# Output weights split in two steps of four, and short side work taken together in one step

## Chip, cores and metric

The kernel runs on one core of one Trainium2 chip. The metric is the device time of one execution in microseconds (us); the median of several executions counts, and lower is better.

## What is computed

One step of a hybrid decoder with one layer: a prompt of 1024 rows and eight single-row decodes (1032 rows together, `NT`). The normalized input is projected by `w_in`; three mixers follow (sparse attention with compressed, selected and window branches, a causal pooling mixer, a gated spatial mixer); each is widened by a SiLU gate; the three outputs are joined and go through one output projection.

```python
def pool_mix(xin, prev, pos0, w_pool, scale):
    ...
    diff = (jnp.concatenate(pooled, axis=-1) - xf[:, POOL_MAX - 1:]).reshape(b, t, N_POOL_GROUPS, POOL_GROUP_DIM)
    y = jnp.einsum('btgc,gce->btge', diff, w_pool).reshape(b, t, D_POOL)
    return y * scale

def merge_groups(x, ya, za, yb, zb, yc, zc, w_out, g_post):
    mix = jnp.concatenate([ya * jax.nn.silu(za), yb * jax.nn.silu(zb), yc * jax.nn.silu(zc)], axis=-1)
    out = jnp.einsum('bte,ed->btd', mix, w_out)
    return x + rms_norm(out, g_post).astype(x.dtype)
```

## The kernel before, in words

Every fp32 operand is split into a high and a low fp16 part, and a product is three matmuls (high by high, low by high, high by low).

The second part of the kernel, from about 205 us on, is one loop over 50 units of attention (`units`, `st` counts the steps). Prompt rows come in tiles of 128 in the order 7, 6, 2, 1, 0, 5, 4, 3 (`ROWS`); a unit is one, two or four heads of a tile. Steps 0 to 7 are tile 7, 8 to 15 tile 6, 16 to 19 tile 2, 20 to 23 tile 1, 24 and 25 tile 0, 26 to 33 tile 5, 34 to 41 tile 4, 42 to 49 tile 3. A step writes, in this order: the scores of its unit (`qk`: matmuls `s`, VectorE's `P` with the row minimum, ScalarE's exponential on `P`, ScalarE's high part `H`), VectorE's low part `L` of the unit before with its DMA transpose (`low`, L1365), the DMA transpose of this unit's `H` (`high`, L1357), one round of the background tasks (`bg_step`), a helping of other work (`take`), and the matmuls `O` with the values for the unit three steps back (`pv`), with `combine` at the end of a half tile and `finish` at the end of a tile.

`take(budget)` draws from two lists. `side` holds `dec_mix`, `gmlp(0)`, `gmlp(1)`, `poolmm(1)`, `poolmm(0)`, `dec_out`; `fill` holds the last groups of the input projection (`tgroup`: ZC1, U1, PIN1, ZB1, PIN0, ZB0, in this order, three chunks of 3.5 each), `early_wo`, `open_out`, and then one `outproj(i)` for each finished tile. Each is a generator that writes a chunk and names its price; the price 0 means that it waits for something. The budget of a step is what is owed (never above 0) plus 6.2 until `open_out` has run, and plus 0.52 times the unit's size after, less 0.19 times the size; the size is 12 in tile 2, 8 in tiles 1, 0 and 3, 11 in tile 5. `take` first draws one chunk of `side`, whatever the budget is, then chunks of `fill` while the budget is above 0 and fewer than two chunks with a PSUM bank to be emptied were drawn. What empties a bank is put in `posts` and written when the next chunk has been written, or at the start of the next step; what comes after it (`fin`) is a background task and goes on in the next `bg_step`. `now` is the planner's own clock, `later` a clock of GpSimd's work on it.

`poolmm(f2)` is one half of the pooled products: three chunks of price 0.45 over 344 columns each, three matmuls `pp` into one bank of the pool `fp`, emptied by VectorE at L1202 into `yzb`; then `fin`: the high part of `mxp` by ScalarE (L1188), the low part by GpSimd (L1189), and `mxp0` or `mxp1` is there. `poolmm(1)` waits for `dh1` (GpSimd's last subtraction of the pooling task `post_pin(1)`, L1171) and for the gate `zb1`; `poolmm(0)` likewise for `dh0` and `zb0`.

`fp` has two banks of PSUM for all this: the groups `ps`, `pp`, `op` (output projection), `oc` (compressed attention, `cmp_out`), `mp` (the transposes in `finish`), `dops` (`dec_out`).

`open_out` runs once ZB0's last chunk is written. It gives back the room of the input, clears a tile on GpSimd (L1447) and starts `split_wo`: seven loads of 512 KB of output weights `wor1` to `wor7` and one of `gpb` on GpSimd's queue (`wor0` came by `early_wo`), then in later rounds the splits `wo`: ScalarE's high part (L1483) and VectorE's low part (L1484). The order of the eight weights is `forder` = 6, 7, 5, 4, 0, 1, 2, 3: 6 and 7 meet `mxg`, 5 meets `mxp1`, 4 meets `mxp0`, 0 to 3 the attention. A weight may be used from the round after its split. `outproj(i)` takes two halves of 512 columns, eight weights by three matmuls `op`; weight 4 goes last where `mxp0` isn't there. While fewer than eight weights are there, each weight is a chunk of 0.65. `dec_out` needs all `mxp`, all weights.

The SP and GpSimd queues are kept in the order of the code (`manual_schedule`); the order on TensorE, VectorE and ScalarE is arranged by the framework at build time.

Of the kernel before, what the change touches and what calls it, by code (L numbers as in the profile page):

```python
# [50 lines left out]
def tile_hymba(ctx: ExitStack, tc: tile.TileContext, A: dict):  # L51
# [40 lines left out]
    def flush():  # L92
        while posts:
            run_post(posts.pop(0))
# [42 lines left out]
    def chunk(gen):  # L137
        r = next(gen, None)
        if r is None:
            return None  # L140
        flush()
        if r[1] is not None:
            posts.append(r[1])
        now[0] += r[0]
        return r[0]
# [454 lines left out]
    def dec_cmp():  # L600
        add_pe(0)
        add_pe(1)
        prep("c", 0)
        yield 0, None
        for b in range(8):
            if b < 6:
                add_pe(b + 2)
            if b < 7:
                prep("c", b + 1)
            else:  # L610
                prep("k", 0)
            hl = chl.pop(("c", b))
            yield compress([(r, hl, r * 512, ms[:, r, b * 8:b * 8 + 8]) for r in range(2)], f"d{b}", f"cd{b}")
# [623 lines left out]
    def small():  # L1237
        yield from small_w()
        for q in range(3):
            nxt_load()  # L1240
        yield 0, None
# [4 lines left out]
    side = [small(), dec_cmp()]  # L1246
# [196 lines left out]
    def open_out():  # L1443
        X.release()
        outp["O"] = tc.alloc_tile_pool(name="O", bufs=1, side="left", reuse_waits="tile")
        outp["one"] = outp["O"].tile([128, 128], F32, name="one2")
        G.memset(outp["one"], 1.0)  # L1447
        bg.append(split_wo())
        yield 0.1, None
# [8 lines left out]
    def load_wo(q):  # L1458
        O = outp.get("O")
        if q == 0:  # L1460
            t = RW.tile([128, 1024], F32, tag="raw", name="wor0", bufs=1)
        elif q < 6:
            t = O.tile([128, 1024], F32, tag=f"w{q + 2}", name=f"wor{q}", bufs=1)
        else:
            t = O.tile([128, 1024], F32, tag="xr", name=f"wor{q}", bufs=2)
        wor[q] = t
        later(0.6)
        G.dma_start(t, A["wo"][forder[q]])

    def split_wo():  # L1470
        for q in range(1, 8):
            load_wo(q)
        outp["gpb"] = outp["O"].tile([128, 1024], F32, name="gpb")
        G.dma_start(outp["gpb"], A["gpb"])
        for part in ((0, 1, 2), (3, 4, 5), (6, 7)):
            yield
            for q in list(outp):
                if q in range(8):
                    wo[forder[q]] = outp.pop(q)
            for q in part:  # L1480
                raw = wor.pop(q)
                w = outp["O"].tile([128, 2, 1024], F16, tag=f"w{q}", name=f"wo{q}", bufs=1)
                S.activation(w[:, 0], raw, AF.Copy, scale=64.0)  # L1483
                V.scalar_tensor_tensor(w[:, 1], raw, 64.0, w[:, 0], ALU.mult, ALU.subtract)  # L1484
                outp[q] = w
        yield
        for q in part:
            wo[forder[q]] = outp.pop(q)
# [118 lines left out]
    side = []  # L1607

    def take(budget):
        banks = 0  # L1610
        c = 0
        while side and c == 0:
            c = chunk(side[0])
            if c is None:
                side.pop(0)
                c = 0
            elif c == 0:
                break
        if c:
            budget -= c  # L1620
            banks = 1
        while budget > 0 and fill and banks < PARAM["banks"]:
            c = chunk(fill[0])
            if c is None:
                fill.pop(0)
                continue
            if c == 0:
                break
            banks += len(posts) > 0
            budget -= c  # L1630
        return min(budget, 0.0)
# [9 lines left out]
    for st in range(n + 3):  # L1641
        t0 = now[0]
        flush()
        u = units[st - 1] if 1 <= st <= n else None
        if st < n:
            pend[units[st]] = qk(units[st])
        if u is not None:
            pend[u] = low(u, *pend[u])
        if st < n:
            pend[units[st]] = high(units[st], *pend[units[st]])  # L1650
        bg_step()
        if st >= n:
            bg_step()
            take(5.2)
        else:
            i, s0, nh = units[st]
            size = nh * (i + 1 + min(i + 1, 5))
            now[0] += 0.19 * size
            owed = take(owed + (PARAM["s2"] * size if "O" in outp else PARAM["s1"]) - 0.19 * size)
            now[0] = max(now[0], t0 + 0.33 * size + 0.8)  # L1660
        if st >= 3:
            v = units[st - 3]
            pv(v, pend.pop(v))
            e = v[1] + v[2]
            if e % 4 == 0:
                run_post(lambda: combine(v[0], v[1] // 4))
            if e == 8:
                fill.append(outproj(v[0]))
    while fill or side:
        flush()  # L1670
        bg_step()
        bg_step()
        take(1.0)
        now[0] += 1.0
# [165 lines left out]
```

## Time and profile before

| | us |
|---|---|
| median of 3 executions | 579.41 |
| the three | 579.08, 579.41, 589.81 |
| the profiled execution | 582.92 |
| its span, first to last instruction | 581.2 |

PE is TensorE's matmuls, PEld its weight loads, DVE is VectorE, ACT ScalarE, POOL GpSimd, SP the queue that issues most DMAs. A row of a timeline has start, duration, engine, line, operation, out<-in with shape, the count of merged instructions, and in brackets the idle time before it and what ended that. Idle times of an engine count only where the engine, or what waits for it, sets the end. Line 67 is the helper that writes every matmul, so matmuls are told apart by their tiles.

### The profile page before, as it was taken

Reading aid. Unit: us, or ns where it says so; the run is one execution under the profiler, and the core shown is the slowest. Engines: PE = TensorE matmul, PEld = TensorE weight load, DVE = VectorE, ACT = ScalarE, POOL = GpSimd, SP = SyncE. Lnnn points to the kernel's source line nnn. Section 1 sums busy time; section 2 is a strip of 40 time slices with the busy share of each in tenths; the row PEclk is TensorE's granted clock in tenths of the full one; section 3 lists DMA queues with packets and bytes.
Section 4 is the critical chain, followed back from the end, with each engine's and each line's share of the span. In section 5 each row is a group of like instructions: output and inputs, shape, how many; then the busy total and the mean of one; then the engine's idle time right before and its main releaser. Section 6 shows DMA issues by size and latency. Waiting matters only on the chain. (4 is left out here: it accounts for less than half of the span.)

```text
span 581.2 us, 14266 instructions
## 1 busy us (share of the span) xinstructions
PE 524.4 (90%) x5748; PEld 347.0 (60%) x5748; DVE 447.1 (77%) x747; ACT 323.4 (56%) x574; POOL 197.5 (34%) x157
## 2 busy tenths in 40 slices
PE   5889989899999999899999888957587999999985
PEld 3556645479877999766666556533345555555452
DVE  5986389998687568469887897869889777888842
ACT  7444144555534434348666666678777566766620
POOL 1894187502266200043937785223000110000000
PEclk9999997999999999999999989975778999999998
DMA  8613984665776111748987588899859899899870
GB/s 297 265 37 111 246 220 126 183 197 160 212 261 178 38 39 21 188 108 172 186 161 143 118 144 149 130 308 156 127 118 143 119 195 200 184 175 204 169 196 36
DMA packets 191125, 93.29 MB, mean 161 GB/s; under 512 B 160458, under 2 KB 179434, under 8 KB 191058
## 3 DMA queue, kind: packets, MB, share of 16 engines
q1 hardware_dynamic: 187170, 78.82, 62.4%
q0 software_dynamic: 3744, 13.29, 7.1%
q8 instruction: 45, 0.74, 0.5%
q10 hardware_dynamic: 144, 0.26, 0.1%
q14 instruction: 22, 0.18, 0.1%
HBM read 45.49 MB, written 11.86 MB: 99 GB/s over the span
## 5 line engine op out<-in xcount | busy, mean ns | idle before, releaser
L67 PE MATMUL ps<-xh,ws 128*128 128x344 f16 x768 | 179.1, 316 | 7.9 <-DVE ws L261 2.6
L67 PEld LDWEIGHTS <-ws 128*128 128x128 f16 x1376 | 129.2, 100 | 90.4 <-issue 16.1
L1348 ACT ACTIVATE P<-P,sm 128x640 f32<-128x640 f32 (+7 forms) x128 | 92.8, 726 | 73.6 <-DVE sm L1346 73.3
L67 PE MATMUL ps<-xl,ws 128*128 128x344 f16 x384 | 121.3, 316 | 0.0
L1364 DVE SCALAR_TENSOR_TENSOR L<-P,H 128x1024 f16<-128x1024 f32 (+4 forms) x50 | 88.8, 1775 | 20.1 <-ACT H L1350 18.5
L1346 DVE CUSTOM_DVE_ANT_0 P<-s,ctt 128x640 f32<-128x640 f32 (+7 forms) x128 | 84.8, 699 | 8.9 <-PE s L67 8.5
L67 PEld LDWEIGHTS <-qa 128*128 128x128 f16 (+1 forms) x612 | 44.7, 98 | 59.6 <-issue 33.5
L67 PE MATMUL O<-vn,T 128*128 128x64 f16 x1584 | 62.2, 197 | 12.3 <-DMA T<-L 8.3
L67 PEld LDWEIGHTS <-T 128*128 128x128 f16 x1584 | 57.4, 101 | 25.2 <-DMA T<-L 9.1
L1350 ACT ACTIVATE H<-P 128x1024 f16<-128x1024 f32 (+4 forms) x50 | 66.2, 1325 | 1.0
L67 PEld LDWEIGHTS <-xh 128*128 128x128 f16 x768 | 60.2, 98 | 0.7
L67 PE MATMUL s<-ka,qa 128*128 128x384 f16 (+4 forms) x192 | 44.2, 330 | 5.0 <-DVE sm L1346 4.7
L67 PE MATMUL op<-wo,qa 128*128 128x512 f16 x192 | 45.1, 381 | 0.5 <-DVE wo L1484 0.5
L67 PE MATMUL zps<-ws,xh 128*128 128x128 f16 x512 | 45.0, 219 | 0.0
L67 PE MATMUL zps<-ws,xl 128*128 128x128 f16 x256 | 43.6, 219 | 0.0
L1514 POOL TENSOR_SCALAR sq<-sq 128x1 f32<-128x1 f32 x8 | 4.2, 528 | 112.1 <-ACT o L1546 112.1
L67 PEld LDWEIGHTS <-xl 128*128 128x128 f16 x384 | 37.5, 98 | 1.1 <-issue 0.5
L255 ACT ACTIVATE ws<-raw 128x1024 f16<-128x1024 f32 x21 | 22.2, 1056 | 17.1 <-PE ps L67 11.9
L67 PE MATMUL s<-klx,qx 64*128 64x384 f16 (+4 forms) x92 | 26.4, 327 | 4.2 <-DMA qx<-qa 4.2
L67 PE MATMUL s<-kl,qa 64*128 64x384 f16 (+5 forms) x100 | 29.1, 334 | 0.0
L67 PE MATMUL op<-wo,mxg 128*128 128x512 f16 x96 | 25.5, 403 | 2.2 <-DVE yzb L1202 2.2
L1073 POOL TENSOR_TENSOR t<-t,yzc 128x1032 f32<-128x1032 f32 x2 | 4.8, 2382 | 61.5 <-DMA qx<-qa 61.0
(335 smaller groups left out, 924.1 us busy)
## 6 DMA issues: line engine op xcount, KB each, us to landing
raw<-in_wt_dram SPq DMA_DIRECT2D x21, 512.0 KB, 4.6
wor<-in_wo_dram POOLq DMA_DIRECT2D x8, 512.0 KB, 9.4
xr<-in_xn_dram SPq DMA_DIRECT2D x8, 512.0 KB, 4.1
o_y_dram<-o SPq DMA_DIRECT2D x7, 512.0 KB, 3.3
cr<-in_ccmp_dram SPq DMA_DIRECT2D x24, 128.0 KB, 2.8
o_kww_dram<-in_cwin_dram POOLq DMA_DIRECT2D x8, 259.0 KB, 4.1
o_kww_dram<-in_cwin_dram POOLq DMA_DIRECT2D x8, 252.0 KB, 4.4
xq<-in_xT_dram SPq DMA_DIRECT2D x3, 516.0 KB, 7.0
```

Of the source, the lines that this page charges most:

```text
L67: nc.tensor.matmul(out, lhsT=l, rhs=r, start=st, stop=en)
L255: S.activation(ws[:, 0, :, a:b], r, AF.Copy, scale=64.0)
L1073: G.tensor_tensor(t, t, hold.pop(f"zc{f2}"), ALU.mult)
L1346: V.tensor_tensor_reduce(p, ps[:, z:z + T], ctt[:, end - T:end], -slope, 3e38, ALU.add, ALU.min, sm[:, s, br:br + 1])
L1348: S.activation(p, p, AF.Exp, bias=sm[:, s, br:br + 1], scale=-1.0, accum_out=sm[:, s, 2 + br:3 + br])
L1350: S.activation(H, P, AF.Copy, scale=1024.0)
L1364: V.scalar_tensor_tensor(L, P, 1024.0, H, ALU.mult, ALU.subtract)
L1514: G.tensor_scalar(sq[:, 2:3], sq[:, 1:2], 1.0 / 1024, sq[:, 0:1], ALU.mult, ALU.add)
```

## The change

`split_wo` splits the weights in two rounds of four instead of three rounds of three, three and two. `take` draws chunks of `side` until their prices reach 1.0, instead of one chunk; a chunk of price 0 ends it as before. Of the side tasks, `gmlp` has chunks of 1.4 and `dec_out` chunks of 2.6, 2.6 and 0.2; only the three chunks of 0.45 of a `poolmm` are short enough to come together.

```diff
-        for part in ((0, 1, 2), (3, 4, 5), (6, 7)):
+        for part in ((0, 1, 2, 3), (4, 5, 6, 7)):
...
-        while side and c == 0:
-            c = chunk(side[0])
-            if c is None:
+        while side and c < 1.0:
+            d = chunk(side[0])
+            if d is None:
                 side.pop(0)
-                c = 0
-            elif c == 0:
+                continue
+            if d == 0:
                 break
+            c += d
```

## Rows read from the trace of the kernel before

**Rows 1.** The page: busy time, share of the span and count of instructions of three engines.

```profile
PE 524.4 (90%) x5748; PEld 347.0 (60%) x5748; DVE 447.1 (77%) x747; ACT 323.4 (56%) x574; POOL 197.5 (34%) x157
```

**Rows 2.** Busy time by stretch: start and end, length, then PE, PEld, DVE, ACT and POOL busy with counts, the granted TensorE clock as a share of full speed, the DMA engines' busy share, GB/s.

```profile
366.00:377.00 11.00, 10.63 (x130) 6.67 (x128) 10.98 (x26) 6.30 (x14) 0.23 (x2) 1.00 0.76 125
377.00:390.00 13.00, 6.19 (x52) 3.92 (x51) 7.55 (x14) 8.16 (x18) 4.17 (x8) 0.74 1.08 283
390.00:413.00 23.00, 17.79 (x165) 9.17 (x166) 22.95 (x52) 19.29 (x44) 6.18 (x3) 0.70 0.91 167
413.00:430.00 17.00, 12.09 (x132) 7.08 (x129) 12.75 (x50) 11.73 (x40) 0.00 (x0) 0.60 0.70 101
430.00:444.00 14.00, 8.93 (x105) 4.76 (x101) 13.86 (x25) 11.96 (x20) 2.15 (x1) 1.00 0.85 166
444.00:454.75 10.75, 10.63 (x208) 7.91 (x207) 9.58 (x19) 7.36 (x14) 1.25 (x1) 0.68 1.15 141
454.75:561.90 107.15, 107.15 (x1073) 57.31 (x1070) 81.75 (x150) 64.30 (x126) 8.19 (x15) 1.00 0.91 180
561.90:581.20 19.30, 10.85 (x44) 4.75 (x42) 6.27 (x10) 1.97 (x5) 0.81 (x2) 0.84 0.23 82
```

**Rows 3.** SP's queue in the timeline: the transpose of H in steps 19, 25 and 28, which mark how far attention is, and the store of the pooling state.

```profile
373.75 0.62 SPq L1163 DMA_DIRECT2D o_ps_dram<-dsh  x1
...
395.05 1.47 SPq L1357 DMA_TRANSPOSE T<-H  x1
...
429.16 1.23 SPq L1357 DMA_TRANSPOSE T<-H  x1
...
443.64 1.66 SPq L1357 DMA_TRANSPOSE T<-H  x1
```

**Rows 4.** The timeline around the first half's pooled products, `poolmm(1)`, and the start of the output projection: matmuls `pp`, `op`, `oc`, VectorE's L1202, the last part of ZB0 (L492).

```profile
367.60 0.61 PE L67 MATMUL pp<-mxp,wpl 128*128 128x344 f16 x3
369.01 3.04 PEld L67 LDWEIGHTS <-ws 128*128 128x128 f16 x22
370.69 0.57 DVE L1202 SCALAR_TENSOR_TENSOR yzb<-pp,psc,yzb 128x344 f32<-128x344 f32 x1
375.79 0.51 DVE L492 SCALAR_TENSOR_TENSOR t<-ps,R 128x344 f32<-128x344 f32 x1
383.33 1.06 PE L67 MATMUL pp<-mxp,wpl 128*128 128x344 f16 x3
387.14 0.63 PE L67 MATMUL pp<-mxp,wpl 128*128 128x344 f16 x3
389.39 0.57 DVE L1202 SCALAR_TENSOR_TENSOR yzb<-pp,psc,yzb 128x344 f32<-128x344 f32 x1
390.01 1.30 PE L67 MATMUL op<-wo,mxg 128*128 128x512 f16 x4 [2.25 <-DVE yzb L1202]
```

**Rows 5.** POOL's queue in the timeline from the pooling task's last work before `open_out` on.

```profile
364.32 1.04 POOL L1141 TENSOR_TENSOR ab<-ab 64x512 f32<-64x512 f32 x1
376.42 0.20 POOL L1447 MEMSET one<- 128x128 f32 x1 [11.07 <-DVE t L492]
376.97 3.68 POOL L1468 DMA_DIRECT2D wor<-in_wo_dram  x7 [0.35 <-PE s L67]
393.70 2.65 POOL L1189 TENSOR_TENSOR mxp<-yzb,mxp 128x1032 f16<-128x1032 f32 x1 [12.53 <-ACT mxp L1188]
396.31 2.66 POOL L1171 TENSOR_TENSOR mxp<-ab,mxp 128x512 f16<-128x512 f32 x1
```

**Rows 6.** DVE in the timeline: `L` of 1536 columns and a split of `wo`, each once without and once with GpSimd at work.

```profile
387.72 1.75 DVE L1364 SCALAR_TENSOR_TENSOR L<-P,H 128x1536 f16<-128x1536 f32 x1
393.17 1.17 DVE L1484 SCALAR_TENSOR_TENSOR wo<-wor,wo 128x1024 f16<-128x1024 f32 x1
394.26 3.69 DVE L1364 SCALAR_TENSOR_TENSOR L<-P,H 128x1536 f16<-128x1536 f32 x1
397.88 2.17 DVE L1484 SCALAR_TENSOR_TENSOR wo<-wor,wo 128x1024 f16<-128x1024 f32 x1
```

**Rows 7.** The three longest idle times of ACT, PE and DVE between 375 and 385 us, in the timeline.

```profile
381.84 0.22 ACT L1162 ACTIVATE dsh<-t 128x8 f32<-128x8 f32 x1 [6.14 <-DMA o_ps_dram<-dsh]
382.11 0.39 PE L67 MATMUL s<-klx,qx 64*128 64x256 f16 x1 [4.21 <-DMA qx<-qa]
384.23 1.23 DVE L1059 SCALAR_TENSOR_TENSOR yzb<-yzb,t 128x1032 f32<-128x1032 f32 x1 [5.42 <-ACT yzb L1056]
```

**Rows 8.** The splits: the two lines over the span (duration least/median/most, first and last start), the time of the loads from issue to landing, and the second and the last of ACT's rows.

```profile
L1483 ACT ACTIVATE wo<-wor x8: 1039/1040/1057, 384.1 to 405.3; 128x1024 f16<-128x1024 f32 x8
L1484 DVE SCALAR_TENSOR_TENSOR wo<-wor,wo x8: 1172/1218/2172, 385.4 to 409.1; 128x1024 f16<-128x1024 f32 x8
DMA to landing us min/median/max: 5.9/9.4/12.0
389.30 1.99 ACT L1483 ACTIVATE wo<-wor 128x1024 f16<-128x1024 f32 x2
```

**Rows 9.** The timeline of the second half's pooled products, `poolmm(0)`, and of what waits for it.

```profile
427.04 1.05 PE L67 MATMUL pp<-mxp,wpl 128*128 128x344 f16 x3
433.25 0.52 DVE L1202 SCALAR_TENSOR_TENSOR yzb<-pp,psc,yzb 128x344 f32<-128x344 f32 x1
433.83 0.82 PE L67 MATMUL oc<-vbd,pct 128*128 128x256 f16 x6 [1.35 <-DVE yzb L1202]
435.01 2.15 POOL L1189 TENSOR_TENSOR mxp<-yzb,mxp 128x1032 f16<-128x1032 f32 x1 [27.61 <-ACT mxp L1188]
436.98 0.38 PE L67 MATMUL op<-wo,mxp 128*128 128x512 f16 x1
444.22 0.35 PE L67 MATMUL dops<-md,wo 128*128 128x16 f16 x8
454.78 1.46 PE L67 MATMUL op<-wo,mxg 128*128 128x512 f16 x6
```

**Rows 10.** The end: the last transpose of L on SP, and the last `O` and the last tile's projection on PE.

```profile
556.37 1.70 SPq L1365 DMA_TRANSPOSE T<-L  x1
561.02 0.81 PE L67 MATMUL O<-vn,T 128*128 128x64 f16 x22
569.50 5.34 PE L67 MATMUL op<-wo,qa 128*128 128x512 f16 x24
```

## The prediction

> **What bounds the kernel now.** I read the page first, then busy time by stretch, then the waits between 370 and 450 us, and at last the timeline there, on SP's and POOL's queues and around every tile that the diff touches. The page calls PE 90% busy [rows 1], an average over three stages. From 454.75 to 561.9 us PE is busy without a gap at the full clock [rows 2]: whatever is left of the output projection then costs its own length. From 377 to 444 PE has gaps: 6.19 of 13, 17.79 of 23, 12.09 of 17, 8.93 of 14 us busy, at a granted clock of 0.60 to 0.74 up to 430 [rows 2]. There VectorE fills 390 to 413 (22.95 of 23 us). After 561.9 the last tile's chain runs alone. So the change, which lies at 367 to 455 us, is worth what it lets PE do in the gaps, and each us gained there reaches the end.
>
> The engines don't keep the code's order: the first pooled product is written in step 19 and ran at 367.60 [rows 4], while SP issued step 19's transpose at 395.05 [rows 3]. Side work runs up to 27 us ahead where its data and one of the two `fp` banks are there. At 427 to 444 it runs level with attention (the products of step 24 and after beside step 25's transpose at 429.16, step 28's `dops` at 444.22 beside its transpose at 443.64) [rows 3, 9].
>
> **The change, part by part.**
>
> *Planner.* Step 18 writes two chunks of ZB0 on a budget of 6.2 - 0.19 x 12 = 3.92, so step 19 owes 3.08 and has 0.84. Before: one product (0.45) leaves 0.39, and ZB0's last chunk is written too. After: three (1.35) leave -0.51; that chunk moves to step 20, whose 6.2 - 1.52 - 0.51 = 4.17 holds it, and `open_out` stays there. `mxp1` comes in the round of step 20 instead of 22. `dh0` stays at step 24 (GpSimd's planned clock reaches 344.49, step 23 starts at 344.19). `poolmm(0)` is then written in step 24 alone instead of 24 to 26; all weights are there at step 24, not 25; `mxp0` at 26 instead of 28. `dec_out` and the end of `outproj(7)`'s first half move from step 28 to 26, and every later piece of the projection stands two steps earlier.
>
> *poolmm(1), 367 to 397 us.* Its products ran at 367.60, 383.33, 387.14; after the last, VectorE's L1202 at 389.39 freed the bank for which `op` waited 2.25 us [rows 4]. All three will now run near 368 to 372. GpSimd's L1189 then stands behind L1141 (ended 365.4) and ahead of the clearing and the seven loads, which ran at 376.42 and 376.97 [rows 5]. It runs near 374 instead of 393.70, and L1171, queued behind it, near 384 instead of 396.31. That frees VectorE: beside those two, an `L` took 3.69 us instead of 1.75 and a split 2.17 instead of 1.17 [rows 5, 6]. 1.94 + 1.00 = 2.9 us leave the stretch in which VectorE is full. The 2.25 us of PE lie in the same stretch and aren't added: **-2.9**. Bounds: -5.1 (both), and 0 (the price moves along, below).
>
> *What that costs at 366 to 379.* VectorE is full there too (10.98 of 11) [rows 2]: it gets two L1202 (2 x 0.57) and what L1189 takes from it. On PE, the third product waits for the first one's bank (freed 371.26, the end of L1202 at 370.69), and ZB0's last chunk, which ran from 369.01, for the next: its end at 375.79 moves by about 2.5 us, and with it the clearing and all loads on POOL [rows 4, 5]. Up to 1.1 + 2.5 = 3.7 us; taken as **0**, since right behind stand idle times of 6.14 us on ACT, 4.21 on PE and 5.42 on DVE [rows 7]. With that cover gone it costs 3.7. It may even gain: the store that ACT waits for was issued at 373.75 [rows 3], 3.2 us ahead of the loads, and took 8 us beside them; with the loads later, those waits may shrink, at most by 4.2.
>
> On a rule against this: the Trainium skill (SBUF — State Buffer, Who interferes with whom) says that a VectorE instruction with two SBUF inputs and a GpSimd one that reads SBUF exclude each other, the later one waiting for the whole of the earlier. By it the price isn't removed but goes with L1189 to its new place, so the term would be about -0.3, not -2.9. The trace shows such a wait in the old place alone.
>
> *The splits.* Still eight by 1.04 us on ACT and 1.2 on DVE [rows 8]: 0 for the work. Four in the first round need `wor3`, the last four `wor7` one round sooner. Loads are issued by 376.97 + 3.68 = 380.65 and take at most 12.0 [rows 5, 8]: landed by 392.7, or 395.2 with the 2.5 us above. The second split ran at 389.30 with no wait for a load, the last at 405.3. The eighth may come at 400; the second may wait. Cost **0**; 2.5 us if ACT stands at the second split until its load lands, with all exponentials behind it.
>
> *poolmm(0), 427 to 455 us.* From the first product to the end of the last L1202: 427.04 to 433.77, 6.7 us, in one bank, because `op` of tile 7 holds the other until `mxp0` [rows 9]. Three products in a row at 0.84 us (mean of the four groups shown: 0.61, 1.06, 0.63 [rows 4], 1.05) plus 0.57 of L1202 are 4.2. `mxp0`, `op` at 436.98 and `dops` follow: **-2.5**. Bounds: 0 (other DVE work still goes between), and -7.3: two steps of tile 5 with 0.33 x 11 = 3.6 of projection each, all done in PE's gaps. `dops` at 444.22 stands behind step 28's work and may now go ahead of it; I take the near end, since the data (`mxp0`) and the bank decide here.
>
> *Sum.* -2.9 + 0 + 0 - 2.5 = -5.4 against the profiled execution: 582.9 - 5.4 = 577.5. That execution stands 3.5 above the median of the runs, so 574.0.
>
> **Rivals.**
>
> *A, swallowed:* the order of work changes and the time doesn't. For it: 427 to 444 is held up by VectorE too (13.86 of 14) [rows 2], and at the end the last `O` (561.02) waits for the transpose issued at 556.37, while `op` of tile 4 fills the wait; projection done earlier leaves that wait empty [rows 10]. The lock rule above ends here as well. Against: PE is full for 107 us before that. Gain 0 to 2: 577.4 to 579.4.
>
> *B, slower:* the weights come late. ZB0's last chunk must wait for two L1202, and the clearing and the loads wait for it on POOL. Price 2.5 us of load plus 2.5 of ACT standing at a split: 584. It decides once the loads start after about 380. For it: the loads saturate DMA (1.08 busy) [rows 2]. Against: the last split had 12 us to spare. Price up to 10 if step 18's transposes fall into the burst anew.
>
> *C, larger:* the waits of rows 7 shrink by 4.2 and PE keeps its clock. From 444 to 454.75 PE is busy 10.63 us at 0.68 [rows 2]; at 1.00 that is 7.2, 3.4 less. 574.0 - 4.2 - 3.4 = 566.4. Against: both need gaps to vanish that have other causes. The Trainium skill (TensorE: Matmul & The Clock Gate, What's actually happening) says the array runs at 1.2 GHz after idling and 2.4 when kept busy; the stretches of rows 2 agree.
>
> *D, no change of order* is excluded: the budget of step 19 alone moves a chunk.
>
> **How the numbers follow.** Forecast, 571 to 577: 0.42. A, 577 to 580: 0.27. B, 580 to 592: 0.19, of it 0.09 above 584. C, 564 to 571: 0.12, of it 0.05 below 567. The likeliest gives 574.0; 567 to 584 leaves out 0.14. Two per cent, about what a measurement can tell from no change, is 11.6 us: below 567.8 lie 0.07, above 591 lie 0.05, between 0.88. The likeliest's own range is 571 to 577, all inside "same".
>
> **What would show it.** Right: three groups of `pp` between 367 and 374; L1189 of the first half ahead of the loads; no `L` of 1536 columns above 3 us after 390; `mxp0`'s L1189 near 432.6; `dops` by 441; the gapless stretch of PE starting about 5 us sooner. Wrong: loads after 380 with ACT idle ahead of a split; the waits of rows 7 as long or longer; a new wait of PE for `T` after 430; or PE idle longer at 556 to 565 by what was gained.

## The result, and the profile after

The changed kernel takes 591.02 us (median of 4 executions, 589.28 to 594.29) where the kernel before takes 581.27 in the same comparison (the three executions of the table and one of 583.13): a ratio of 1.0144, interval 1.0102 to 1.0186, or +8.4 us. The forecast was 574.0, range 567 to 584: wrong in sign, and outside the range. The profiled execution of after took 590.38 us (span 588.6). Differences below are ratio less one, times the median of before in the same comparison. Of one experiment, `first_price`, the profile fell into a stretch of lower clock and is not read; its repeat is.

The page of the changed kernel, the line that answers to [rows 1]: PE's busy time has not grown (520.2 us against 524.4), the time around it has.

```profile
PE 520.2 (88%) x5748; PEld 345.6 (59%) x5748; DVE 444.6 (76%) x747; ACT 322.5 (55%) x574; POOL 190.6 (32%) x157
```

Busy time by stretch in the changed kernel, columns as in [rows 2], the last stretch reaching to the new end:

```profile
366.00:377.00 11.00, 8.86 (x115) 5.17 (x113) 10.14 (x24) 9.13 (x19) 0.20 (x1) 1.00 0.91 128
377.00:390.00 13.00, 7.62 (x66) 5.16 (x67) 7.77 (x26) 7.12 (x19) 2.15 (x1) 0.74 0.89 111
390.00:413.00 23.00, 10.25 (x138) 6.49 (x137) 15.56 (x36) 15.28 (x34) 5.73 (x11) 0.76 1.00 268
413.00:430.00 17.00, 14.69 (x148) 7.93 (x146) 16.94 (x52) 12.48 (x36) 0.00 (x0) 0.90 0.75 84
454.75:561.90 107.15, 105.45 (x1071) 56.73 (x1069) 82.30 (x152) 67.40 (x132) 6.19 (x14) 1.00 0.91 181
561.90:588.60 26.70, 13.20 (x89) 6.87 (x87) 8.74 (x12) 1.98 (x5) 0.81 (x2) 0.76 0.29 79
```

Against [rows 2], two stretches stand out. From 390 to 413 PE does 10.25 us of work instead of 17.79 and VectorE 15.56 instead of 22.95, while the DMA engines move 268 GB/s instead of 167: the loads of the weights have come into this stretch from the one before (111 GB/s instead of 283). And the last stretch is 26.7 us long instead of 19.3, for 13.2 us of PE work.

Why the loads came late is in the timeline of the changed kernel between 368 and 399 us, PE, ScalarE and GpSimd:

```profile
368.44 0.61 PE L67 MATMUL pp<-mxp,wpl 128*128 128x344 f16 x3
369.88 0.60 PE L67 MATMUL pp<-mxp,wpl 128*128 128x344 f16 x3
374.70 0.60 PE L67 MATMUL pp<-mxp,wpl 128*128 128x344 f16 x3
375.13 0.82 PE L67 MATMUL oc<-vbd,pct 128*128 128x256 f16 x6
382.84 0.21 ACT L1162 ACTIVATE dsh<-t 128x8 f32<-128x8 f32 x1 [6.18 <-DMA o_ps_dram<-dsh]
382.96 1.04 ACT L1188 ACTIVATE mxp<-yzb 128x1032 f16<-128x1032 f32 x1
383.91 0.67 ACT L1382 ACTIVATE ocs<-oc,rsc 128x512 f32<-128x512 f32 x1
384.15 2.15 POOL L1189 TENSOR_TENSOR mxp<-yzb,mxp 128x1032 f16<-128x1032 f32 x1 [17.95 <-ACT mxp L1188]
386.37 1.09 PE L1431 MATMUL mp<-ident,yza 128*128 128x128 f32 x4
387.05 3.99 PEld L67 LDWEIGHTS <-ws 128*128 128x128 f16 x24
393.67 0.20 POOL L1447 MEMSET one<- 128x128 f32 x1 [7.38 <-DVE t L492]
394.20 3.68 POOL L1468 DMA_DIRECT2D wor<-in_wo_dram  x7 [0.33 <-issue]
```

The three products came in a row, as forecast. But ZB0's last chunk (the 24 weight loads from `ws`) did not follow them: `oc` and `mp` took the `fp` banks first. `oc` was emptied by ScalarE's L1382 only at 383.91, because ScalarE stood for 6.18 us at L1162. So the chunk began at 387.05 instead of 369.01 [rows 4], and the loads of the output weights at 394.20 instead of 376.97 [rows 5]: 17.2 us later, not 2.5.

What the late loads met, on SP's queue and PE (the bracket is PE's wait):

```profile
394.92 1.45 SPq L1365 DMA_TRANSPOSE T<-L  x1
401.71 3.98 SPq L1357 DMA_TRANSPOSE T<-H  x1
406.39 3.91 SPq L1284 DMA_DIRECT2D qx<-qa  x2
```
```profile
410.06 0.82 PE L67 MATMUL O<-vn,T 128*128 128x64 f16 x12 [9.85 <-DMA T<-L]
```

The transpose of L issued at 394.92 stands 0.7 us behind the first load. PE's `O` waited 9.85 us for it, until 410.06; the longest such wait before, from 360 to 470, was 3.9.

How far attention is, told by SP's transpose of H (start in us, steps counted from 0 as in the code), for before, after and three of the experiments below:

| step | before | after | after_held | zb0_first | zb0_first_held |
|---|---|---|---|---|---|
| 0 | 259.31 | 260.00 | 261.54 | 260.10 | 260.81 |
| 20 | 399.85 | 393.41 | 394.69 | 400.08 | 398.72 |
| 24 | 419.80 | 427.46 | 429.23 | 417.46 | 416.79 |
| 27 | 440.15 | 444.80 | 446.61 | 436.57 | 436.45 |
| 29 | 449.23 | 453.91 | 456.79 | 447.24 | 446.06 |
| 30 | 455.27 | 462.67 | 462.72 | 457.72 | 452.19 |
| 35 | 485.03 | 494.09 | 491.00 | 490.74 | 480.48 |
| 49 | 554.47 | 561.86 | 559.50 | 558.57 | 549.87 |

After is 6.4 us ahead of before at step 20: ScalarE wrote the H of step 18 (L1350) at 375.18, ahead of its long stand at L1162, and in before only at 385.65, behind it. It is 7.7 behind at step 24, 4.7 at step 29, 7.4 at step 30 and 7.4 at step 49. So there are two places where attention falls behind, steps 21 to 24 and step 30; from there on the distance stays between 5.7 and 9.1.

The second half's products and what follows them, in the timeline of the changed kernel (answering to [rows 9]):

```profile
418.21 0.61 PE L67 MATMUL pp<-mxp,wpl 128*128 128x344 f16 x3
423.09 0.61 PE L67 MATMUL pp<-mxp,wpl 128*128 128x344 f16 x3
426.29 0.61 PE L67 MATMUL pp<-mxp,wpl 128*128 128x344 f16 x3
428.49 0.34 PE L67 MATMUL dops<-md,wo 128*128 128x16 f16 x8 [0.74 <-DVE yzb L1202]
430.00 2.14 POOL L1189 TENSOR_TENSOR mxp<-yzb,mxp 128x1032 f16<-128x1032 f32 x1 [30.26 <-ACT mxp L1188]
432.37 1.04 PE L67 MATMUL op<-wo,mxp 128*128 128x512 f16 x2
```

`dops` now starts ahead of `op`, at 428.49 instead of 444.22: `dec_out` is early, while attention is late. The end, PE in the timeline (answering to [rows 10]):

```profile
565.29 0.23 PE L67 MATMUL O<-vn,T 128*128 128x64 f16 x2 [2.18 <-DMA T<-H]
567.45 1.35 PE L67 MATMUL O<-vn,T 128*128 128x64 f16 x22 [1.93 <-DMA T<-L]
...
576.92 5.34 PE L67 MATMUL op<-wo,qa 128*128 128x512 f16 x24
```

The last `O` stands 6.4 us later than before and waits for its transposes with nothing to fill the wait; the last 24 matmuls of the projection start 7.4 us later, as far as attention is behind. Nearly all of the loss is idle time of PE: from 450 us to the end PE stood idle for 15.2 us in the changed kernel and 8.5 in before, and the profiled spans are 7.4 apart.

### The profile page after: what moved, and what is told of

Same layout as the page of the kernel before. It is cut to its first block, busy times and chain, and to the rows that moved or that the text cites. A ratio compares the mean times of both kernels' runs of the same rounds, so it can differ in the third digit from the quotient of the medians.

```text
span 588.6 us, 14266 instructions
## 1 busy us (share of the span) xinstructions
PE 520.2 (88%) x5748; PEld 345.6 (59%) x5748; DVE 444.6 (76%) x747; ACT 322.5 (55%) x574; POOL 190.6 (32%) x157
## 5 line engine op out<-in xcount | busy, mean ns | idle before, releaser
L67 PE MATMUL ps<-xh,ws 128*128 128x344 f16 x768 | 177.2, 314 | 9.3 <-DVE t L492 4.6
L1364 DVE SCALAR_TENSOR_TENSOR L<-P,H 128x1024 f16<-128x1024 f32 (+4 forms) x50 | 85.9, 1718 | 19.3 <-ACT H L1350 15.8
L67 PE MATMUL O<-vn,T 128*128 128x64 f16 x1584 | 62.5, 196 | 27.5 <-DMA T<-L 19.3
L1350 ACT ACTIVATE H<-P 128x1024 f16<-128x1024 f32 (+4 forms) x50 | 66.2, 1324 | 0.9
L67 PE MATMUL s<-ka,qa 128*128 128x384 f16 (+4 forms) x192 | 42.7, 321 | 2.6 <-DVE sm L1346 2.4
L1514 POOL TENSOR_SCALAR sq<-sq 128x1 f32<-128x1 f32 x8 | 2.6, 331 | 125.1 <-ACT o L1546 125.1
L255 ACT ACTIVATE ws<-raw 128x1024 f16<-128x1024 f32 x21 | 22.2, 1056 | 18.6 <-PE ps L67 13.2
L261 DVE SCALAR_TENSOR_TENSOR ws<-raw,ws 128x1024 f16<-128x1024 f32 x16 | 22.1, 1381 | 5.6 <-ACT ws L255 5.6
```

Of the source, the lines that this page charges most:

```text
L67: nc.tensor.matmul(out, lhsT=l, rhs=r, start=st, stop=en)
L255: S.activation(ws[:, 0, :, a:b], r, AF.Copy, scale=64.0)
L261: V.scalar_tensor_tensor(ws[:, 1, :, a:b], r, 64.0, ws[:, 0, :, a:b], ALU.mult, ALU.subtract)
L1350: S.activation(H, P, AF.Copy, scale=1024.0)
L1364: V.scalar_tensor_tensor(L, P, 1024.0, H, ALU.mult, ALU.subtract)
L1514: G.tensor_scalar(sq[:, 2:3], sq[:, 1:2], 1.0 / 1024, sq[:, 0:1], ALU.mult, ALU.add)
```

## The experiments

Theory 1: ZB0's last chunk is put off by a step, and the late loads cost. Theory 2: the splits in blocks of four cost. Theory 3: `dec_out` and the projection, written two steps earlier, cost. Each kernel was timed beside the kernel before.

**Halves of the change.** `split_only` is before with the new `part` line alone. `group_only` is after with the old `part` line.

> The kernel before with the splits in two rounds of four; the pooled products stay one in a step. Theory 1 (the loss is the delay of ZB0's last chunk by a step, which puts it behind cmp_out's `oc` and finish's `mp` in the two-bank pool, and with it the clearing and the seven loads 17 us later): the chunk runs at 369 and the loads at 377 as before, time within 1.5 us of the kernel before. Theory 2 (the longer blocks of splits on ScalarE and VectorE): 6 to 10 us slower than before, most of the loss. Theory 3 (the projection stands two steps earlier and is missing as filler at the end): the projection's place hardly moves, so within 1.5 us of before.

> The kernel after with the splits in three rounds of three, three and two as before; the products stay grouped. Theory 1: loads at 394 as in the changed kernel, time 588 to 592, 7 to 11 us above before. Theory 2: the loss is gone, within 2 us of before. Theory 3: the projection is as early as in the changed kernel, 588 to 592.

Measured: `split_only` 1.0025 [0.9983, 1.0067], loads at 378.42; `group_only` 1.0157 [1.0113, 1.0202], loads at 394.17. The split shows no cost (its interval ends at +3.9 us); theory 2 falls, and the grouping alone gives a loss as large as that of the whole change.

**Late loads without the change.** `zb0_late` is before with one price altered:

```diff
-            yield 0.45, done
+            yield (1.35 if f2 == 1 and c == 0 else 0.45), done
```

> The kernel before, products one in a step and splits in three rounds, but the first product of the first half is priced 1.35, so that step 19's budget is overdrawn and ZB0's last chunk is written one step later, in step 20 (open_out in step 21). Theory 1: the chunk runs behind `oc` and `mp`, loads at 392 or later, time 588 to 594 with neither the grouping nor the split of four. Theory 2: splits in blocks of three, within 2 us of before. Theory 3: the projection comes later than before, not earlier, so no slower than before by more than 2 us.

Measured: 1.0118 [1.0055, 1.0182], +6.9 us, with ZB0's chunk at 392.01 behind `oc` and `mp`, the loads at 398.49 and a wait of PE for a transpose of L of 10.0 us. As theory 1 says. But its expectation is wrong in one point: here `dec_out` and the second half of tile 7's projection come one step earlier as well (27), not later, so this run alone does not tell theory 1 from theory 3.

**The loads early again, the rest as changed.** `first_price` (and its repeat `first_price_b`) charges a group with its first chunk alone:

```diff
-            c += d
+            c = c or d
+            got += d
```

> The changed kernel, but a group of side chunks is charged to the step's budget with the price of its first chunk alone (0.45 instead of 1.35). ZB0's last chunk is then written in step 19 again, right behind the three products and ahead of `oc` and `mp`; open_out in step 20; splits, poolmm(0), dec_out and the projection stand as in the changed kernel. Theory 1: loads at 378 to 381, PE's wait of 9.9 us for a transpose of L near 400 to 410 is gone, time 575 to 583, that is at or below before. Theory 2 and theory 3: nothing that they blame is changed, 588 to 592.

> The kernel first_price again for an undisturbed profile. Theory 1: ZB0's last chunk ends near 377, but the clearing and the loads stand behind L1189 on GpSimd, which waits for ScalarE's L1188 at 383, so that the loads start at 385 to 387; their stretch then falls on steps 19 to 21, with waits of PE for T of 5 us or more there.

Measured: 1.0211 [1.0157, 1.0264], no faster than the changed kernel, where theory 1 had it at or below before. But the loads came at 385.06 (profile of `first_price_b`, 593.44 us), behind L1189 on GpSimd. `loads_first` adds a hold to L1189 for that reason:

```diff
+            while "gpb" not in outp:
+                yield
             G.tensor_tensor(mxp[:, f2, 1], y, mxp[:, f2, 0], ALU.subtract)
```

> The kernel first_price once more, and GpSimd's L1189 of the first half held back until the seven loads are issued (in first_price it stood ahead of them and waited for ScalarE, so that they came some 8 us late all the same, on top of a disturbed profile). ZB0's last chunk still stands behind the three products. Theory 1 (late loads make the loss): loads at 379 to 382, no wait of PE for a transpose above 5 us between 385 and 430, time 577 to 584. Theory 2 (splits in blocks of four): excluded by now. Theory 3 (the projection stands two steps earlier): 587 to 594, as in the changed kernel. Theory 4 (the three products in a row ahead of `oc` and of the scores hold attention up, wherever the loads are): 587 to 594.

`zb0_first` is after with that hold and ZB0's chunk ahead of the products:

```diff
         banks = 0
         c = 0
+        if st == 19:
+            budget -= chunk(fill[0])
```

> The changed kernel, but in step 19 ZB0's last chunk is written ahead of the three grouped products instead of behind them, and L1189 of the first half is held back until the loads are issued. Theory 1: the chunk ends by 373, loads at 374 to 377, time 574 to 582. Theory 3 (projection two steps earlier): 587 to 594. Theory 4 (three products in a row ahead of `oc`): 585 to 592.

`group_p0` is before with the grouping for the second half alone (the rest of the loop as in the change):

```diff
-        while side and c == 0:
+        while side and c < (1.0 if "mxp1" in hold else 0.1):
```

> The kernel before with only the second half's products, poolmm(0), in one step; the first half's stay one in a step, the splits in three rounds. This is the second term of the prediction alone (-2.5 us) and with it the projection and dec_out two steps earlier. Loads at 377 as before. Prediction's term: 577 to 580 where before gives 581. Rival A (swallowed at the end): 580 to 582. Theory 3 (projection two steps earlier is what costs): 586 to 592.

Measured: `loads_first` 1.0277 [1.0231, 1.0323] with loads at 380.03; `zb0_first` 1.0177 [1.0135, 1.0218] with loads at 377.25; `group_p0` 1.0186 [1.0143, 1.0230], loads at 381.87, as early as before for its own start. Theory 1 missed the two for which it named a time, and `group_p0` loses as much with its loads in their old place: with early loads the loss is no smaller. Theory 3 hit `zb0_first` and came within 0.1 us of its range in `group_p0` (592.09). `loads_first`, at 594.9 us, lies above the range of every theory, and it is no clean test: PE waited 11.0 us for a transpose of L there, until 396.78, which theory 1 had excluded. In `zb0_first` the longest such wait from 360 to 440 was 3.7 us.

**Theory 3 alone.** The hold gives the word that `mxp0` is there in step 28, as in the kernel before. With it `dec_out` and every chunk of the projection from there on are written in the steps of before:

```diff
+            while f2 == 0 and st < 28:
+                yield
             hold[f"mxp{f2}"] = 1
```

`p0_held`, `after_held` and `zb0_first_held` are `group_p0`, after and `zb0_first` with it. `after_s49` is after with the planner's share 0.49 instead of 0.52.

> The kernel group_p0 (second half's products in one step, everything else as before), and the word that mxp0 is there is given only in step 28, as in the kernel before, so that dec_out and every piece of the projection from there on are written in the same steps as before. What is left of the change is poolmm(0) in one step. Theory 3 (what costs is that dec_out and the projection stand two steps earlier): 577 to 583, the loss of group_p0 is gone. Theory 5 (three products of the second half in a row cost by themselves): 588 to 593.

> The changed kernel with the same hold: mxp0 is given in step 28, dec_out and the projection from step 28 on stand as before; the grouping, the split in fours and the late loads (394) stay. Theory 3: 577 to 583, the whole loss gone, though the loads are 17 us late. Theory 1 (late loads cost by themselves): 586 to 592. Both add, each with a half: 583 to 586.

> The kernel zb0_first (changed kernel with ZB0's last chunk ahead of the products and loads at 377) with the same hold to step 28. Neither of the two suspected costs is left, and the grouping is in place for both halves. Theory 3 alone, or theory 3 with theory 1: 574 to 581, the 2.9 us of GpSimd's lock may show as a gain. Theory 4 (three products in a row hold attention up): 585 to 592.

> The changed kernel with the planner's share of a step for other work cut from 0.52 to 0.49, nothing else. The projection starts as early as in the changed kernel (dec_out in step 26) but is spread thinner, so that tile 4's chunks are written in steps 48, 49, 50 and 50, as in the kernel before, instead of 45, 47, 47 and 48. Theory 3a (the loss is the filler that is missing behind the last steps of attention): 577 to 583. Theory 3b (the loss is projection written ahead of the attention of steps 26 to 30): 586 to 592. Theory 1 (late loads): 586 to 592.

Measured: `p0_held` 0.9974 [0.9945, 1.0003]; `after_held` 1.0056 [1.0020, 1.0092]; `zb0_first_held` 0.9952 [0.9914, 0.9990], faster than both kernels; `after_s49` 1.0102 [1.0060, 1.0144], or 587.7 us, in the range of theories 3b and 1 and outside that of 3a. `after_held`, at 585.3, hit the forecast that both add. The hold is worth 12.3 us between `group_p0` and `p0_held`, 13 between `zb0_first` and its held twin, and 5.1 in the changed kernel. What is left in `after_held`, 3.3 us, falls to the late loads by elimination. The groups of three products cost nothing by themselves, neither in the first half (`zb0_first_held`) nor in the second (`p0_held`): theories 4 and 5, which the expectations name for them, fall.

The twins `zb0_first` and `zb0_first_held` are level at step 27 (0.12 us apart) and 8.7 apart at step 49. PE in the timeline of `zb0_first` from the last scores ahead of the projection to the next:

```profile
448.41 0.33 PE L67 MATMUL s<-klx,qx 64*128 64x384 f16 x1
448.68 0.61 PE L67 MATMUL O<-vn,T 128*128 128x64 f16 x15
449.12 1.46 PE L67 MATMUL op<-wo,mxg 128*128 128x512 f16 x6
...
456.89 2.75 PE L67 MATMUL op<-wo,qa 128*128 128x512 f16 x12
459.48 0.43 PE L67 MATMUL s<-ka,qa 128*128 128x320 f16 x2
```

and of `zb0_first_held`:

```profile
449.35 0.44 PE L67 MATMUL s<-ka,qa 128*128 128x320 f16 x2
449.72 0.31 PE L67 MATMUL s<-kl,qa 64*128 64x320 f16 x1
449.73 0.31 PE L67 MATMUL s<-klx,qx 64*128 64x320 f16 x1
449.96 0.23 PE L67 MATMUL O<-vn,T 128*128 128x64 f16 x2
450.03 1.46 PE L67 MATMUL op<-wo,mxg 128*128 128x512 f16 x6
...
456.51 1.46 PE L67 MATMUL op<-wo,mxp 128*128 128x512 f16 x6
457.80 0.83 PE L67 MATMUL O<-vn,T 128*128 128x64 f16 x23
458.47 0.76 PE L67 MATMUL s<-ka,qa 128*128 128x384 f16 x4
```

Cut at `...` are further `op`, without a gap. The projection starts at 449.12 in the one and 450.03 in the other: written two steps earlier, it ran 0.9 us earlier. What changed is what stands behind it. In `zb0_first` the scores of 320 columns that complete the unit come after both halves, 10.4 us behind the start of the projection (459.48). In its twin they were done ahead of it (449.35), and VectorE and ScalarE have work from them meanwhile. Busy time from 450 to 460 shows it, columns as in [rows 2]:

```profile
450.00:460.00 10.00, 10.00 (x50) 4.71 (x49) 5.37 (x10) 2.95 (x6) 2.49 (x3) 1.00 0.67 116
```
```profile
450.00:460.00 10.00, 10.00 (x73) 4.82 (x72) 7.82 (x13) 5.45 (x10) 1.73 (x3) 1.00 0.64 120
```

The first is `zb0_first`, the second its twin: VectorE 5.37 against 7.82 us, ScalarE 2.95 against 5.45, PE full in both. The late scores are those of step 31: ScalarE wrote its H (L1352) at 464.15, and SP transposed it at 465.54; in the twin these are 453.45 and 458.70.

Step 30 is late for another reason, which is on ScalarE and SP of `zb0_first`:

```profile
447.24 1.37 SPq L1359 DMA_TRANSPOSE T<-H  x1
449.54 1.38 ACT L1352 ACTIVATE H<-P 128x1408 f16<-128x1408 f32 x1
453.55 0.36 SPq L1600 DMA_DIRECT2D o_yd_dram<-do  x1
457.72 1.73 SPq L1359 DMA_TRANSPOSE T<-H  x1
```

Its H was ready by 451, from scores ahead of the projection. But SP stood 4.9 us for VectorE's last work on `do`, to store the result of `dec_out`, and this store, written early like `dec_out`, stands ahead of the transpose in SP's queue; in the twin the transpose went at 452.19 and the store at 461.28. This delay can be made up: `zb0_first_mid` (below) stood 7.0 us for the same store, had step 30 at 464.45, and was 2.7 us ahead of `zb0_first` at step 35.

PE being full in both, the price is not paid in this stretch. From 450 us to the end, columns as in [rows 2], first `zb0_first`, then its twin:

```profile
450.00:585.40 135.40, 120.47 (x1107) 63.47 (x1105) 89.64 (x161) 67.53 (x133) 8.97 (x17) 0.95 0.75 156
```
```profile
450.00:575.50 125.50, 116.91 (x1120) 61.47 (x1118) 88.27 (x159) 67.34 (x133) 9.45 (x17) 0.99 0.82 168
```

PE stood idle for 14.9 us in the one and 8.6 in the other, all of it after 530, and was busy 3.6 us longer at a granted clock of 0.95 instead of 0.99: together the 9.9 us between the spans. `group_p0` (15.2) and `p0_held` (8.6) stand apart in the same way. That the projection spent early is then missing beside an attention that is behind fits this; it is not shown by itself.

**Which end of the shift.** Two steps earlier also means that tile 4's chunks are written in steps 45 to 48 instead of 48 to 50, so that they are missing behind attention's last steps. Theory 3a puts the loss there, theory 3b to the projection ahead of the scores of steps 26 to 30. `zb0_first_mid` draws no projection in steps 28 and 29 (first edit), `zb0_first_tail` holds tile 4's back to step 48 (second edit; `last` lists the tiles' projections), `zb0_first_h27` and `zb0_first_h30` have the hold at 27 and 30:

```diff
         while budget > 0 and fill and banks < PARAM["banks"]:
+            if st in (28, 29):
+                break
...
+            if st in (45, 46, 47) and fill[0] is last[-1]:
+                break
```

> The kernel zb0_first (projection and dec_out from step 26), but nothing is drawn from the projection's list in steps 28 and 29; its pair of chunks of tile 7 then stands in step 30, as in the kernel before, and tile 4's in 48, 49, 50, 50. dec_out stays two steps early. Theory 3b (the stretch of projection ahead of the scores of steps 29 and 30 costs): 576 to 582. Theory 3a (the filler missing at the end costs): 576 to 582 too, since the end is put right as well. If dec_out's early place costs: 585 to 592.

> The kernel zb0_first, but the projection of tile 4 (the last but one) is not drawn before step 48, so that its four chunks stand in steps 48, 48, 49 and 50 instead of 45, 47, 47 and 48; everything before that as in zb0_first, with the early pair in step 28. Theory 3a: 576 to 583. Theory 3b: 585 to 592.

> The kernel zb0_first with mxp0 given in step 27: dec_out and the projection one step earlier than in the kernel before, not two and not none. Theory 3b: the pair stands in step 29, in the middle of tile 5's units like that of step 28, so most of the loss stays: 584 to 592. Theory 3a: one chunk more at the end than in zb0_first, half of the loss: 581 to 586.

> The kernel zb0_first with mxp0 given in step 30: dec_out and the projection two steps later than in the kernel before. Theory 3a: the filler at the end is there with a chunk to spare, but six chunks stand behind attention's last step instead of four; 2.6 us of them may lengthen the end: 577 to 584. Theory 3b: the pair of tile 7 stands in step 32, more attention has gone ahead; 574 to 582.

Measured: `zb0_first_mid` 1.0030 [0.9996, 1.0063]; `zb0_first_tail` 1.0139 [1.0071, 1.0207]; `zb0_first_h27` 1.0180 [1.0112, 1.0247]; `zb0_first_h30` 1.0046 [1.0004, 1.0088]. Keeping the projection out of steps 28 and 29, which puts the end right as well, takes most of the loss away, 8.5 of 13 us. The 4.5 us that stay are not assigned; `dec_out` and its store are still early there. Mending the end alone gives 2.2 us, less than its interval, and PE stood as long as in `zb0_first` from 450 on (14.8 us, of it 4.0 before 550). So between the two it is theory 3b. One step early costs as much as two, but not in the same way: in the profile of `zb0_first_h27` attention is level with before at step 49 (554.70 against 554.47), and the time is lost behind it, which neither theory forecast. Two steps late is no gain: attention was then 8.6 us ahead of before at step 49, and the time was given back to the projection left behind it.

## Why the prediction was wrong

**The step that failed: the two steps by which the projection moves.** The prediction worked out rightly that `dec_out` and every later piece of the projection stand two steps earlier, and counted that as nothing or as a gain of up to 7.3 us, two steps of 3.6 in PE's gaps. It never asked what would stand behind those pieces, on PE and on SP. That is the side on which it counts: 12 to 13 us where the loads are early, 5.1 in the changed kernel. "Each us gained there reaches the end" was kept in one profiled execution: `zb0_first_held` is 4.5 us ahead of before at step 35 and 4.6 at step 49 (its gain over all executions is 2.8). But PE being busy without a gap was read as PE being indifferent to the order of its work. From 450 to 460 a gapless PE left VectorE 2.5 us less to do in `zb0_first` than in its twin, and after 530 PE stood 6.3 us longer.

**The second step that failed: "its end at 375.79 moves by about 2.5 us".** Its L492 came at 393.10, 17.3 us later. I counted the two banks that the chunk must wait for among the products alone. Being written in step 20 put it behind what is written in between: `oc` at the end of step 19, and `mp` in step 20 ahead of `take`. And the cover that I named for a delay, ScalarE's 6.14 us of idle time [rows 7], is the wait that held `oc`'s bank: it was no cover but a link of the chain. Rival B had the mechanism (loads after 380, at 0.19). Its price was put together from a wait of ScalarE at a split, which was 1.1 us, and not from the transposes, which it only named as "up to 10". That 591.02 lies in its range of 580 to 592 is in part luck, since 5.1 of the 8.4 us come from the shift, which it did not have.

What this delay is worth by itself: `after_held` against `zb0_first_held`, 6 us, or 3.3 above before. The two losses don't add: `zb0_first`, with early loads, is no faster than the changed kernel. Why the shift costs 13 us in one setting and 5 in the other is not settled. The longest stretch without scores does not tell it: 10.7 us in `zb0_first`, 7.7 in the changed kernel (449.1 to 456.8), but 8.4 in before and in `zb0_first_held`, which lose nothing. SP's stand for the store of `dec_out` was 4.9 us in `zb0_first` and 0.8 in the changed kernel, which goes the same way, but `zb0_first_mid` had 7.0 and lost little.

**-2.9 at 390 to 413.** The mechanism was right. In the changed kernel no `L` of 1536 columns and no split ran beside L1189:

```profile
389.56 1.75 DVE L1364 SCALAR_TENSOR_TENSOR L<-P,H 128x1536 f16<-128x1536 f32 x1
397.30 1.22 DVE L1484 SCALAR_TENSOR_TENSOR wo<-wor,wo 128x1024 f16<-128x1024 f32 x1
```

against 3.69 and 2.17 in [rows 6]. In the changed kernel VectorE was no longer what filled the stretch (15.56 of 23 us), so it could buy little there; no run tells this term apart. By the lock rule weighed in the prediction, the price would have gone along with L1189. In the trace it did not: at 384.15 to 386.30 VectorE stood idle, waiting for ScalarE. Where L1189 of the second half landed on VectorE's work it was there again: L1425 at 430.39 took 2.29 us, where the median of that line is 0.69. L1189 itself came at 384.15 and not near 374, again for ScalarE's stall.

**-2.5 for `poolmm(0)`.** The products did not close up. From the first of them to the end of the last L1202 took 6.7 us in before, 7.0 in `group_p0` and 10.2 in the changed kernel, not 4.2. In `p0_held` they ran at 427.13, 429.09 and 431.99, in the places of before (427.04, 428.98, 431.66), though written in one step: the second waited 0.42 us for the L1202 of the first, and VectorE is full there (19.86 of 20 us from 430 to 450). So the bound of 0 was the one to take. `p0_held` itself gives -1.5 us, interval -3.2 to +0.2, but with the hold `op` and `dops` could not follow sooner, so it does not test that part of the term. In the changed kernel they did, `dops` 15.7 us sooner, and it is the slower one.

**The splits at 0** held (`split_only`). **The waits of rows 7** stayed as long without any load beside them (6.18 us on ScalarE at 382.84): the loads did not cause them, and rival C had no ground. **Rival A's** empty wait at the end is real: it is where the profiles show the loss. But `zb0_first_tail` shows that filling it does not cure it. **The clock:** two stretches of [rows 2] do not bear out what I read from them, for from 430 to 444 PE was busy 8.93 of 14 us at a granted clock of 1.00, and from 444 to 454.75 10.63 of 10.75 at 0.68.

**The forecast of what would show it** named, for wrong, loads after 380 with ScalarE idle ahead of a split, which came (394.20, and 1.07 us), and a new wait for `T` after 430; the long one came earlier, at 400 to 410. But of the signs for right some came too: L1189 ahead of the loads, no `L` of 1536 columns above 3 us after 390, `dops` by 441. They followed single pieces, and the gap was in the sum, which had no term for attention.

## What to carry to other kernels

When a change moves filler to an earlier step, ask for each piece what then stands behind it in the queue of its engine, and whether the other engines have work to live on that long; an engine that is busy without a gap doesn't answer that. Ask the same of its stores in the queue of SP. What filler costs shows where it is missing later, so compare the idle time to the end as well. When a chunk slips by a step, list everything that the new step writes ahead of it and takes from the same buffers, and follow each buffer to the engine that frees it. An idle time is cover only if nothing that the delayed work needs is waiting behind it.

## What was not expected of the hardware

- A transpose of L issued 0.7 us behind the first of the seven loads of 512 KB took 15.1 us to land (394.92 to 410.06, changed kernel); the transposes issued from 380 to 420 had medians of 5.2 (H) and 5.7 us (L).
- SP's own issue of a transpose took 3.98 us beside the loads (401.71) and of two copies 3.91 (406.39), where 1.27 (411.77) and 1.25 (419.98) came right after. In `loads_first` the issue of one transpose of L, 1.0 us behind the first load, took 11.15 us (381.07).
- Starts of the second part differ by up to 6.1 us between profiled executions (258.6 to 264.8 at step 0), and part of a late start is made up by step 26 (`group_p0`: +5.5 at step 0, +1.1 at step 26 against before). Why was not tried.
